# Gate and up products of a hybrid decoder trunk: eight quarter products per column tile, or seven by Strassen's scheme

## The chip, the cores and the metric

The kernel runs on one core of a Trainium2 chip (trn2). The metric is the device time of one execution in microseconds. Before the change it is 2174.89 us, the median of three runs (2173.87 to 2179.53).

## The reference

Two layers (DEPTH = 2) over 512 tokens of width 1024. Each layer runs two feed-forward blocks, a mixing sub-layer between them and a per-layer embedding at the end; the change touches the feed-forward blocks alone.

```python
def swiglu(x, wg, wu, wd):
    return (jax.nn.silu(x @ wg) * (x @ wu)) @ wd
...
#  h += 1/2 * post(SwiGLU_1(pre(h)))      pre and post: RMSNorm with a gain
#  h += post(mixing(pre(h)))
#  h += 1/2 * post(SwiGLU_2(pre(h)))
#  h += post(sigmoid(pre(h) @ W_g) * (p[i] @ W_p))
```

wg and wu are 1024 x 2816, wd is 2816 x 1024, all float32.

## The kernel before

Everything is kept transposed: channels in the 128 partitions, the 512 tokens in the columns. A product of float32 matrices is made of three products in the type float32r: each operand is split into a rounded high part and a rest, low part (`split`, `split_w`: ScalarE copies the high part, VectorE subtracts it), and `mm3` adds high x high, high x low and low x high in one PSUM bank.

A feed-forward block (`ffn`) has 22 column tiles (FT) of 128 hidden channels. For each tile, `gate_up` makes the gate and the up product: 8 row blocks (KD) of 128 channels times three partial products, 24 matmuls into a bank of the tag "mm" (four banks), for gate and up 48. The first three tiles are made in two token halves of 256 columns, so that they can start before the second half of the tokens is normalised; tiles 3 to 21 are 512 columns wide. The norm's gain is in the operand (`high`, `low`: xh, xl), its per-token scale r2 is put on the results afterwards, in `evacuate`: VectorE multiplies gate and up by r2 (L548, L550), ScalarE takes silu (L549), VectorE multiplies the two (L551) and the hidden tile is split for the next product (hh, hl: L200, L201). `evacuate` of a tile is called while the next tiles' matmuls run (`later`, `both`). Then `down` multiplies the 22 hidden tiles by wd into 8 output tiles, the last two again in token halves.

The weights come through `Weights`: chunks of 128 x 1024, eight 128 x 128 blocks, in one fixed list (`order`), a 512 KB DMA each from SyncE's queue (L55) into one of three buffers "raw", split by ScalarE (L185: wh) and VectorE (L186: wl) in two pieces of 512 columns, 12 buffers for each part. `part` calls `advance`, which runs four chunks ahead. A feed-forward block takes 44 chunks of gate and up (one of gate, one of up per tile, tiles in order) and 22 of down.

The order of the work is partly written by hand. Matmuls stay in program order (`in_order`), and after each of them chains that wait (norms, evacuations) go a step on when their time has come. `pin` and `front` keep the weight splits in order on ScalarE and VectorE. The rest is set by a scheduler at build time.

Of the kernel before, what the change touches and what calls it, by code (L numbers as in the profile page):

```python
# [20 lines left out]
FT = 22  # L21
HALF = 256
# [9 lines left out]
class Weights:  # L32
    """Streams [128, 1024] chunks of eight [128, 128] blocks and splits each into two float32r parts."""

    def __init__(self, kern, order, ahead):
        self.kern = kern
        self.order = order
        self.pos = {key: i for i, key in enumerate(order)}
        self.ahead = ahead
        self.issued = 0  # L40
        self.closed = {f"wo{l}" for l in range(L)}
        self.parts = {}
        self.base = None

    def advance(self, upto):
        k = self.kern
        while self.issued < min(upto, len(self.order)):
# [4 lines left out]
            raw = k.p_raw.tile([128, 1024], F32, tag="raw", name="raw")  # L52
            src = k.dram[name]
            if width == 512:
                self.last = k.nc.sync.dma_start(raw, src[c])  # L55
            else:
                self.last = k.nc.sync.dma_start(raw[:, :count * width], src[:, 3 * width * c:3 * width * c + count * width])
            part = []
            for i in range(count):
                if name.startswith("pp"):  # L60
                    hi, lo = (k.slot("big", n, dt=F32R) for n in ("pph", "ppl"))
                else:
                    hi = k.pool.tile([128, width], F32R, tag="wh", name="wh", bufs=12)
                    lo = k.pool.tile([128, width], F32R, tag="wl", name="wl", bufs=12)
                k.split_w(raw[:, width * i:width * i + width], hi, lo)
                part.append((hi, lo))
            self.parts[name, c] = part
            self.issued += 1

    def halves(self, name, c):  # L70
        """The two token halves, while the chunks from this one on have to stay for the second half."""
# [27 lines left out]
class Kern:  # L99
    def __init__(self, tc, ctx, dram, out):  # L100
        self.tc, self.nc, self.dram, self.out = tc, tc.nc, dram, out
        self.pool = ctx.enter_context(tc.tile_pool(name="sb", bufs=1))
        self.p_raw = ctx.enter_context(tc.tile_pool(name="raw", bufs=3))
# [3 lines left out]
        for l in range(L):  # L107
            order += [(f"gu{l}0", c) for c in range(44)] + [(f"dn{l}0", c) for c in range(22)]
            order += [(f"wi{l}", c) for c in range(8)] + [(f"wav{l}", c) for c in range(2)]
            order += [(f"wvg{l}", c) for c in range(3)] + [(f"wi{l}", c) for c in range(8, 14)] + [(f"wo{l}", c) for c in range(8)]  # L110
            order += [(f"gu{l}1", c) for c in range(44)] + [(f"dn{l}1", c) for c in range(22)]
# [9 lines left out]
        self.busy = False  # L121

# [10 lines left out]
    def after(self, ins, prev):  # L133
        """Keeps an instruction that is ready early from taking its tile long before it is needed."""
# [10 lines left out]
    def mm(self, out, lhs, rhs, start, stop):  # L145
        n = math.prod(out.shape[1:])
        self.in_order(self.nc.tensor.matmul(out, lhs, rhs, start=start, stop=stop),  # L147
# [5 lines left out]
    def in_order(self, ins, cycles):  # L153
        """Keeps the products in program order and lets waiting chains go on after each."""
# [23 lines left out]
    def drive(self, mark):  # L178
        """Emits the waiting chains up to a mark."""
# [3 lines left out]
    def split_w(self, src, hi, lo):  # L183
        """Never ahead of a step of a chain, or of an evacuation, that came before it."""
        for engine, ins in (("s", self.nc.scalar.activation(hi, src, AF.Copy)),  # L185
# [3 lines left out]
            self.pin(engine, ins, self.strict)  # L189

# [48 lines left out]
    def bias_table(self):  # L239
# [11 lines left out]
        ps = self.bank("o")  # L251
        self.mm(ps[:8], rb, oh, True, True)
        nc.vector.tensor_copy(row, ps[:8])
        ps = self.bank("o")
# [51 lines left out]
    def high(self, l, n, k, rng):  # L306
        """First float32r part of h times the norm's gain; the per-token scale follows the product."""
# [25 lines left out]
    def square_into(self, acc, src, last=False):  # L333
        """acc: the sum of the squares, and at the very end a last square that the product over the channels adds."""
# [16 lines left out]
    def start(self):  # L351
        """Loads x by pieces, in the order in which the first products need it and their weights."""
# [71 lines left out]
    def put_f(self, l, n, m, src, rng, square_first=False):  # L424
        """src None: the branch is there already, without the gain."""
# [12 lines left out]
    def finish(self, i, nxt, gain=None):  # L438
        """Adds the normalised branch to h over one token half, then prepares the next projection's operand."""
# [48 lines left out]
    def last_half(self, fs, bc, a, b):  # L488
        """The end of the last branch, with one pair of channel tiles on GpSimd."""
# [34 lines left out]
    def ffn(self, l, j, n_post, nxt):  # L524
# [57 lines left out]
        for mark in late:  # L582
            self.drive(mark)
# [671 lines left out]
```

## Time and profile before

| | |
|---|---|
| time, median of 3 runs | 2174.89 us |
| profiled execution: span, first to last instruction | 2176.8 us |
| profiled execution: own time | not given beside the span |
| PE busy (matmuls) | 2134.8 us, 98% |
| PE weight loads (PEld) | 1845.2 us, 85% |
| DVE (VectorE) busy | 1099.8 us, 51% |
| ACT (ScalarE) busy | 935.7 us, 43% |
| POOL (GpSimd) busy | 283.5 us, 13% |
| granted TensorE clock, mean | 0.995 of 2.4 GHz |
| DMA | 196.92 MB, 90 GB/s |

Busy time is the union of an engine's rows. Matmuls are pipelined, and a row lasts longer than the time until the next one starts; the price of a matmul is therefore read from the distance of starts. A weight load goes with each matmul and runs beside the one before. The chain of waits follows the end of the program back, at each step to what released it.

### The profile page before, as it was taken

To read this page: it belongs to the slowest core of one execution; us is meant where nothing else is said; L and a number is where in the kernel's file an instruction comes from. 1 tells how busy PE (TensorE), PEld (TensorE's weight loads), DVE (VectorE), ACT (ScalarE), POOL (GpSimd) and SP (SyncE) were. 2 spreads that over 40 slices of the span, in tenths; PEclk is the share of its full clock that TensorE was granted. 3 is DMA by queue.
4 is the path that set the end of the run, shared out by engine and by line. 5 is a ranking of instruction groups with operands and counts; after the bars stand their busy time and mean duration, and the time that the engine had idled before them with its cause. 6 is when DMAs were issued, how large, how long until landed. Compare 5 with 4: busy or idle time off the path is not lost.

```text
span 2176.8 us, 31253 instructions
## 1 busy us (share of the span) xinstructions
PE 2134.8 (98%) x12152; PEld 1845.2 (85%) x12152; DVE 1099.8 (51%) x2109; ACT 935.7 (43%) x1977; POOL 283.5 (13%) x392
## 2 busy tenths in 40 slices
PE   8999999999999999999999999999999999999998
PEld 7878888988989888889988888899989988888897
DVE  8444422767546444324774443246774564443264
ACT  5333322576744333324553333245675543333254
POOL 2000001312131000002320000022021410000032
PEclk9999999999999999999999999999999999999999
DMA  5342322441013232222232222324300232222221
GB/s 175 100 136 97 97 87 78 138 136 49 1 49 109 95 97 95 90 87 93 74 107 97 97 89 86 107 74 142 126 30 11 69 107 89 95 97 89 95 88 40
DMA packets 60684, 196.92 MB, mean 90 GB/s; under 512 B 6566, under 2 KB 10831, under 8 KB 60536
## 3 DMA queue, kind: packets, MB, share of 16 engines
q1 hardware_dynamic: 60536, 194.93, 27.5%
q8 instruction: 96, 1.57, 0.3%
q14 instruction: 52, 0.43, 0.1%
HBM read 192.78 MB, written 4.74 MB: 91 GB/s over the span
## 4 chain that ended last, share of the span: by engine, by line
PE 89%; DVE 5%; issue 2%; ACT 2%; POOL 1%; DMA 1%; DVEq 0%; SPq 0%; POOLq 0%; ACTq 0%
PE mm L147 80%; PE o L147 7%; PE t L151 2%; DVE wl L186 1%; PE t L147 1%; DVE xl L314 1%; DVE h L472 1%; POOL acc L344 0%; DMA raw<-in_pg 0%; DVE f L463 0%; ACT p L1115 0%; DVE f L466 0%; ACT wh L185 0%; POOL rs L299 0%; ACT xh L309 0%
## 5 line engine op out<-in xcount | busy, mean ns | idle before, releaser
L147 PE MATMUL mm<-xh,wh 128*128 128x512 f32 (+1 forms) x2112 | 753.3, 357 | 8.8 <-ACT wh L185 7.9
L147 PE MATMUL mm<-xl,wh 128*128 128x512 f32 (+1 forms) x2112 | 752.8, 356 | 6.9 <-DVE xl L314 6.8
L147 PE MATMUL mm<-xh,wl 128*128 128x512 f32 (+1 forms) x2112 | 751.3, 356 | 2.6 <-DVE wl L186 2.6
L186 DVE TENSOR_TENSOR wl<-raw,wh 128x512 fp32r<-128x512 f32 (+1 forms) x672 | 464.2, 706 | 543.3 <-ACT wh L185 541.6
L185 ACT ACTIVATE wh<-raw 128x512 fp32r<-128x512 f32 (+1 forms) x672 | 408.6, 631 | 629.6 <-PE mm L147 603.6
L147 PEld LDWEIGHTS mm<-xl,wh 128*128 128x128 f32 x2112 | 401.3, 190 | 71.5 <-DVE xl L314 10.7
L147 PEld LDWEIGHTS mm<-xh,wh 128*128 128x128 f32 x2112 | 401.3, 190 | 70.4 <-ACT wh L185 8.3
L147 PEld LDWEIGHTS mm<-xh,wl 128*128 128x128 f32 x2112 | 400.6, 190 | 64.7 <-DVE wl L186 3.7
L344 POOL TENSOR_TENSOR acc<-acc,sq 128x256 f32<-128x256 f32 x209 | 176.5, 855 | 1477.8 <-ACT sq L340 1473.5
L147 PE MATMUL mm<-hh,wh 128*128 128x512 f32 (+1 forms) x880 | 307.6, 350 | 0.0
L147 PE MATMUL mm<-hl,wh 128*128 128x512 f32 (+1 forms) x880 | 307.0, 349 | 0.0
L147 PE MATMUL mm<-hh,wl 128*128 128x512 f32 (+1 forms) x880 | 307.0, 349 | 0.0
L147 PEld LDWEIGHTS mm<-hl,wh 128*128 128x128 f32 x880 | 166.2, 189 | 24.2
L147 PEld LDWEIGHTS mm<-hh,wh 128*128 128x128 f32 x880 | 165.4, 188 | 24.1
L147 PEld LDWEIGHTS mm<-hh,wl 128*128 128x128 f32 x880 | 165.3, 188 | 23.9
L433 ACT ACTIVATE f<-mm,cols 128x256 f32<-128x256 f32 x96 | 46.2, 481 | 273.3 <-PE mm L147 273.2
L548 DVE TENSOR_TENSOR silu<-mm,r 128x512 f32<-128x512 f32 (+1 forms) x100 | 62.6, 626 | 129.9 <-PE mm L147 124.8
L550 DVE TENSOR_TENSOR up<-mm,r 128x512 f32<-128x512 f32 (+1 forms) x100 | 62.6, 626 | 125.6 <-PE mm L147 125.1
L200 ACT ACTIVATE hh<-silu 128x512 fp32r<-128x512 f32 (+1 forms) x100 | 57.8, 580 | 113.6 <-DVE silu L551 113.6
L314 DVE SCALAR_TENSOR_TENSOR xl<-h,cols,xh 128x256 fp32r<-128x256 f32 x128 | 85.4, 707 | 5.8 <-PE mm L147 3.6
L201 DVE TENSOR_TENSOR hl<-silu,hh 128x512 fp32r<-128x512 f32 (+1 forms) x100 | 62.4, 626 | 49.6 <-ACT hh L200 49.5
L1115 ACT ACTIVATE p<-p,mx 128x512 f32<-128x512 f32 (+3 forms) x128 | 70.3, 554 | 18.0 <-DVE mx L1111 18.0
(231 smaller groups left out, 2201.5 us busy)
## 6 DMA issues: line engine op xcount, KB each, us to landing
raw<-in_gu SPq DMA_DIRECT2D x176, 512.0 KB, 3.3
raw<-in_dn SPq DMA_DIRECT2D x88, 512.0 KB, 3.3
raw<-in_wi SPq DMA_DIRECT2D x28, 512.0 KB, 3.3
raw<-in_wo SPq DMA_DIRECT2D x16, 512.0 KB, 4.3
raw<-in_pg SPq DMA_DIRECT2D x16, 512.0 KB, 4.4
cw<-in_cw SPq DMA_DIRECT2D x16, 256.0 KB, 7.2
bias<-brow SPq DMA_DIRECT2D x16, 256.0 KB, 5.0
raw<-in_pp SPq DMA_DIRECT2D x6, 512.0 KB, 3.9
```

Of the source, the lines that this page charges most:

```text
L147: self.in_order(self.nc.tensor.matmul(out, lhs, rhs, start=start, stop=stop), n if lhs.dtype == F32R and n >= 256 else 4 * n)
L151: self.in_order(self.nc.tensor.transpose(out, src, self.ident), 256)
L185: for engine, ins in (("s", self.nc.scalar.activation(hi, src, AF.Copy)), ("v", self.nc.vector.tensor_sub(lo, src, hi.bitcast(F32)))):
L186: ("v", self.nc.vector.tensor_sub(lo, src, hi.bitcast(F32)))):
L200: nc.scalar.activation(hi, src, AF.Copy)
L201: nc.vector.tensor_sub(lo, src, hi.bitcast(F32))
L314: return self.nc.vector.scalar_tensor_tensor(lo, self.h[:, k, a:b], self.g[:, l, n, k:k + 1], hi.bitcast(F32), op0=OP.mult, op1=OP.subtract)
L344: nc.gpsimd.tensor_add(acc[0], acc[0], q)
L433: self.front["s"] = nc.scalar.activation(f, s, AF.Copy, scale=self.g[:, l, n, m:m + 1])
L548: nc.vector.tensor_mul(s, gu[0], r2[:, a:b])
L550: nc.vector.tensor_mul(u, gu[1], r2[:, a:b])
L1115: self.nc.scalar.activation(a["p"][i], a["p"][i], AF.Exp, bias=a["mx"][:, i:i + 1], accum_out=a["sm"][:, i:i + 1])
```

## The change

Tiles 6 to 21 (NC = 6) of each feed-forward block leave `gate_up` and go through `strassen`. For a column tile, gate above up is a matrix of two by two quarters: A11 and A12 are gate's row blocks 0 to 3 and 4 to 7, the lower pair are up's. The operand has quarters too: row blocks 0 to 3 or 4 to 7, token half left or right. Instead of eight quarter products, each 4 row blocks x 3 partial products of 256 columns, there are seven: A11 x B11, A12 x B21, S1 x t1, S2 x t2, S3 x T3, S4 x B22 and A22 x T4, where S, t and T are sums and differences of quarters (Winograd's form).

- `right_forms` makes the right-hand forms once per block, in the first six tiles, when the second token half's scale is there: h times gain times r2, complete, so that the per-token scale needs no place afterwards; then four differences per row-block pair and 14 splits in all, on VectorE and ScalarE (bh, bl).
- `Weights.form` replaces a tile's two chunk splits: loads of gate (g) and up (u), in steps "s1" and "s2" four additions of 512 columns on VectorE (L93: into y, u, y and z), then splits of g, y, u (1024 columns each) and z (512).
- `strassen` runs a tile's products interleaved with those of the tile before: A11(f), S4(f-1), A22(f-1), S2(f), A12(f), S3(f), S1(f). A tile has three half-filled banks: a ("mm"), b (one of the two "o" banks, in turn) and c ("mm"). ScalarE copies a into b after A11 (L764), so that S2, S1 and S4 add to it; b is read between them: after S2 (L781, up's left half), after S1 (L790, up's right half) and after S4 (L768, silu of gate's right half). Silu of gate's left half comes from a after A12 (L784). c gets S3, is added to up's right half (L791), then takes A22 x T4 and is added to up's left half (L772). L774 multiplies gate and up (up has its sign turned) into the hidden tile. Two one-matmul products per block write both b banks first.
- `evacuate` no longer splits the hidden tile. `split_hid` does it later: four tiles during `strassen`, 18 at the start of the down products, whose first two output tiles (`first_pair`) are now made row block by row block together.
- Buffers: eight of 1024 columns for raw chunks, y and all low parts ("raw"), six of 1024 for the high parts ("wh").

Where the instructions now stand: VectorE, a tile in the middle of the gate/up stage of a block, before (wl: low part of a weight piece; L548 to L551 and L201 as above):

```order
L186 TENSOR_TENSOR wl<-raw,wh 128x512
L548 TENSOR_TENSOR silu<-mm,r_99 128x512
L186 TENSOR_TENSOR wl<-raw,wh 128x512 x2
L550 TENSOR_TENSOR up<-mm,r_99 128x512
L186 TENSOR_TENSOR wl<-raw,wh 128x512
L551 TENSOR_TENSOR silu<-silu,up 128x512
L201 TENSOR_TENSOR hl<-silu,hh 128x512
```

and with the change:

```order
L93 TENSOR_TENSOR raw<-raw 128x512 x2
L791 TENSOR_TENSOR uv<-uv,mm 128x256
L93 TENSOR_TENSOR raw<-raw 128x512
L93 TENSOR_TENSOR sz<-raw 128x512
L250 TENSOR_TENSOR raw<-raw,wh 128x1024 x2
L772 TENSOR_TENSOR uv<-uv,mm 128x256
L774 SCALAR_TENSOR_TENSOR s<-uv,sg 128x512
L250 TENSOR_TENSOR raw<-raw,wh 128x1024
L250 TENSOR_TENSOR zl<-sz,zh 128x512
```

Eight instructions became eleven, and two of them (L791, L772) wait for products in the middle of the additions and splits for coming tiles.

ScalarE at the same place, before:

```order
L185 ACTIVATE wh<-raw 128x512 x2
L200 ACTIVATE hh<-silu 128x512
L185 ACTIVATE wh<-raw 128x512 x2
L549 ACTIVATE silu<-silu 128x512
L185 ACTIVATE wh<-raw 128x512 x4
```

and with the change:

```order
L790 ACTIVATE uv<-o 128x256
L764 ACTIVATE o<-mm 128x256
L249 ACTIVATE wh<-raw 128x1024
L249 ACTIVATE zh<-sz 128x512
L768 ACTIVATE sg<-o 128x256
L249 ACTIVATE wh<-raw 128x1024
L781 ACTIVATE uv<-o 128x256
L249 ACTIVATE wh<-raw 128x1024
L784 ACTIVATE sg<-mm 128x256
```

The copies that PE waits for (L764 before S2, L781 before S1, L790 before S4) stand between copies of high parts that wait for loads and additions.

SyncE's queue at the end of the first block's gate/up loads, before, with what each DMA waits for:

```order
L55 DMA raw_1603<-in_gu00 128x1024 [waits DMAHW6_49,DMAHW3_49,DVE_49]
L55 DMA raw_1648<-in_gu00 128x1024 [waits DMAHW4_49,DVE_49]
L55 DMA raw_1683<-in_gu00 128x1024 [waits DMAHW5_49,DVE_49]
L55 DMA raw_1728<-in_gu00 128x1024 [waits DMAHW6_49,DVE_49]
L55 DMA raw_1763<-in_gu00 128x1024 [waits DMAHW7_49,DVE_49]
```

and with the change:

```order
L82 DMA raw_2447<-in_gu00 128x1024 [waits DMAHW1_49,DVE_49]
L82 DMA raw_2568<-in_gu00 128x1024 [waits PE_49]
L82 DMA raw_2570<-in_gu00 128x1024 [waits DMAHW3_49,DVE_49]
L82 DMA raw_2691<-in_gu00 128x1024 [waits DMAHW0_49,PE_49]
L82 DMA raw_2693<-in_gu00 128x1024 [waits DMAHW5_49,DVE_49]
```

Loads of g (raw_2568, raw_2691) now wait for PE, loads of u (raw_2570, raw_2693) for VectorE. In the built program u's chunk takes the buffer of y of the tile before, once that y is split, and g's chunk one that a low part or the g of an earlier tile leaves.

The diff, cut to its core:

```diff
+NC = 6
...
+    def form(self, name, f, piece):
...
+        if piece == "load":
+            src = k.dram["gu" + name[2:]]
+            self.parts[name, f] = dict(g=self.fetch(src[2 * f]), u=self.fetch(src[2 * f + 1]))
+            return
...
+        if piece == "s1":
+            p["y"] = self.raw()
+            add(p["y"][:, lo], u[:, lo], u[:, hi])
+            add(u[:, lo], u[:, lo], g[:, lo])
+        elif piece == "s2":
+            p["z"] = k.slot("scr", "sz")
+            add(p["y"][:, hi], u[:, lo], u[:, hi])
+            add(p["z"], p["y"][:, hi], g[:, hi])
+        else:
...
+            last = k.split_w(t, h, low)
...
+    def ffn_order(l, j):
+        order = [(f"gu{l}{j}", c) for c in range(2 * NC)] + [(f"gs{l}{j}", (NC, "load"))]
+        for f in range(NC, FT):
+            order += [(f"gs{l}{j}", (f, piece)) for piece in ("s1", "s2", "g", "y")]
+            if f + 1 < FT:
+                order.append((f"gs{l}{j}", (f + 1, "load")))
+            order += [(f"gs{l}{j}", (f, piece)) for piece in ("u", "z")]
...
-            nc.vector.tensor_mul(s, s, u)
-            self.split(s, hid[f][0][:, a:b], hid[f][1][:, a:b])
+            nc.vector.tensor_mul(whole[f][:, a:b], s, u)
...
-        for f in range(3, FT):
+        for f in range(3, NC):
+            if f == NC - 2:
+                self.w.ahead = 9
             both(f, FULL)
...
-        for m in range(6):
+        self.strassen(l, j, forms, whole, split_hid)
+        first_pair()
+        for m in range(2, 6):
             down(m, FULL)
...
+    def right_forms(self, me, r2, forms):
...
+        for k in range(4):
+            a, b, c = (self.slot("big", "b") for _ in range(3))
...
+            times(a, k)
+            times(b, k + 4)
+            nc.vector.tensor_sub(c[:, left], b[:, right], a[:, right])
+            nc.vector.tensor_sub(a[:, right], a[:, left], a[:, right])
...
+            parts(a, ("B11", k), ("t1", k))
+            yield 2.0
+            parts(c, ("T3", k), ("t2", k))
+            parts(b, ("B21", k), ("B22", k))
...
+    def strassen(self, l, j, forms, whole, split_hid):
...
+        for b in shared:
+            p = w.parts[name, NC]
+            self.mm(b, p["A11"][0][:, :128], forms["B11"][0][0], True, True)
...
+                product(cur["a"], cur["p"], "A11", "B11", True)
+                nc.scalar.activation(cur["b"], cur["a"], AF.Copy)
+                pace(0)
+            if prev:
+                product(prev["b"], prev["p"], "S4", "B22")
+                nc.scalar.activation(prev["sg"][:, right], prev["b"], AF.Silu)
+                if cur:
+                    pace(1)
+                product(prev["c"], prev["p"], "A22", "T4")
+                nc.vector.tensor_add(prev["uv"][:, left], prev["uv"][:, left], prev["c"])
+                s = self.slot("big", "s")
+                nc.vector.scalar_tensor_tensor(s, prev["uv"], -1.0, prev["sg"], op0=OP.mult, op1=OP.mult)
...
+                product(cur["b"], cur["p"], "S2", "t2")
+                nc.scalar.activation(cur["uv"][:, left], cur["b"], AF.Copy)
+                pace(3)
+                product(cur["a"], cur["p"], "A12", "B21")
+                nc.scalar.activation(cur["sg"][:, left], cur["a"], AF.Silu)
+                pace(4)
+                cur["c"] = self.bank("mm")[:, :HALF]
+                product(cur["c"], cur["p"], "S3", "T3", True)
+                pace(5)
+                product(cur["b"], cur["p"], "S1", "t1")
+                nc.scalar.activation(cur["uv"][:, right], cur["b"], AF.Copy)
+                nc.vector.tensor_add(cur["uv"][:, right], cur["uv"][:, right], cur["c"])
...
-            a[f"dn{l}{j}"] = _blocks(ffn_w_down[l, j])
+            a[f"dn{l}{j}"] = _blocks(ffn_w_down[l, j], 2)
```

`pace(i)` sends the next piece of the weights' list (a load, an addition step or a split) after a product.

## Rows read from the trace of the kernel before

**Rows 1.** The page: busy time, share of the span and instructions of each engine.

```profile
PE 2134.8 (98%) x12152; PEld 1845.2 (85%) x12152; DVE 1099.8 (51%) x2109; ACT 935.7 (43%) x1977; POOL 283.5 (13%) x392
```

**Rows 2.** The page: the chain that ended last, shares by engine and by line.

```profile
PE 89%; DVE 5%; issue 2%; ACT 2%; POOL 1%; DMA 1%; DVEq 0%; SPq 0%; POOLq 0%; ACTq 0%
PE mm L147 80%; PE o L147 7%; PE t L151 2%; DVE wl L186 1%; PE t L147 1%; DVE xl L314 1%; DVE h L472 1%; POOL acc L344 0%; DMA raw<-in_pg 0%; DVE f L463 0%; ACT p L1115 0%; DVE f L466 0%; ACT wh L185 0%; POOL rs L299 0%; ACT xh L309 0%
```

**Rows 3.** Busy time by stretch: PE, PEld, DVE, ACT, POOL (instructions), granted clock, DMA share, GB/s.

```profile
629.00:647.00 18.00, 18.00 (x161) 18.00 (x160) 10.14 (x16) 10.31 (x28) 9.21 (x10) 1.00 0.13 42
676.00:720.00 44.00, 43.82 (x239) 37.57 (x240) 23.81 (x41) 18.03 (x32) 0.13 (x1) 1.00 0.39 131
800.00:930.00 130.00, 130.00 (x559) 104.75 (x558) 54.99 (x84) 41.02 (x68) 0.00 (x0) 1.00 0.29 94
```

**Rows 4.** Groups by shape: count | busy us, mean ns of one | idle before, releaser.

```profile
L147 PE MATMUL mm<-xh,wh 128*128 128x512 f32 x1344 | 532.7, 396 | 0.0
L147 PEld LDWEIGHTS mm<-xh,wh 128*128 128x128 f32 x2112 | 401.3, 190 | 70.4 <-ACT wh L185 8.3 <-DVE silu L548 1.1 <-issue 0.7
L186 DVE TENSOR_TENSOR wl<-raw,wh 128x512 fp32r<-128x512 f32 x656 | 457.8, 713 | 540.0 <-ACT wh L185 538.3
L185 ACT ACTIVATE wh<-raw 128x512 fp32r<-128x512 f32 x656 | 402.5, 636 | 625.4 <-PE mm L147 599.5 <-DMA raw<-in_pg 7.7 <-DMA raw<-in_gu 7.4
L548 DVE TENSOR_TENSOR silu<-mm,r 128x512 f32<-128x512 f32 x76 | 52.6, 692 | 123.5 <-PE mm L147 123.5
L551 DVE TENSOR_TENSOR silu<-silu,up 128x512 f32<-128x512 f32 x76 | 52.2, 686 | 0.0
L549 ACT ACTIVATE silu<-silu 128x512 f32<-128x512 f32 x76 | 48.1, 633 | 19.3 <-DVE silu L548 19.3
L551 DVE TENSOR_TENSOR silu<-silu,up 128x256 f32<-128x256 f32 x24 | 10.5, 442 | 0.3
L548 DVE TENSOR_TENSOR silu<-mm,r 128x256 f32<-128x256 f32 x24 | 10.1, 420 | 6.4 <-ACT r L322 4.8 <-PE mm L147 1.3
L549 ACT ACTIVATE silu<-silu 128x256 f32<-128x256 f32 x24 | 9.9, 413 | 7.9 <-DVE silu L548 7.6 <-ACT wh L185 0.2
```

**Rows 5.** Timeline of DVE, second block: start us, us, instruction [idle before].

```profile
693.42 0.69 DVE L548 TENSOR_TENSOR silu<-mm,r 128x512 f32<-128x512 f32 x1 [1.68 <-PE mm L147]
...
704.62 0.69 DVE L548 TENSOR_TENSOR silu<-mm,r 128x512 f32<-128x512 f32 x1 [1.63 <-PE mm L147]
...
715.82 0.69 DVE L548 TENSOR_TENSOR silu<-mm,r 128x512 f32<-128x512 f32 x1 [1.63 <-PE mm L147]
```

**Rows 6.** Timeline of PE before the second block, first and eleventh of eleven starts.

```profile
639.78 0.28 PE L147 MATMUL mm<-yh,wl 128*128 128x256 f32 x1
...
640.91 0.28 PE L147 MATMUL mm<-yh,wh 128*128 128x256 f32 x1
```

**Rows 7.** The chain of waits near the end of the program: start us, us.

```profile
2142.04 2.83 PE mm L147 x24
```

**Rows 8.** Timeline of ACT: the second half's scale r in the second block.

```profile
676.93 0.38 ACT L322 ACTIVATE r<-t 128x256 f32<-128x256 f32 x1 [0.59 <-PE t L147]
```

**Rows 9.** Timeline of DVE without pauses, four weight splits merged.

```profile
651.93 3.01 DVE L186 TENSOR_TENSOR wl<-raw,wh 128x512 fp32r<-128x512 f32 x4
```

**Rows 10.** The page: DMA issues, count, KB each, median us to landing.

```profile
raw<-in_gu SPq DMA_DIRECT2D x176, 512.0 KB, 3.3
...
raw<-in_pg SPq DMA_DIRECT2D x16, 512.0 KB, 4.4
cw<-in_cw SPq DMA_DIRECT2D x16, 256.0 KB, 7.2
```

**Rows 11.** Waits of PE: us in total, times, longest.

```profile
PE o L147 <- ACT pj L636: 1.5, 2, 0.8
```

More of the change, by code (lines that the diff above doesn't have):

```diff
@@ L51, in advance @@
             width, count = (280, 2 if c == 2 else 3) if name.startswith("wvg") else (512, 2)
-            raw = k.p_raw.tile([128, 1024], F32, tag="raw", name="raw")
+            if name.startswith("gs"):
+                self.form(name, *c)
+                self.issued += 1
+                continue
             src = k.dram[name]
[L54 to L57, printed above, removed]
+            raw = self.fetch(src[c]) if width == 512 else self.fetch(
+                src[:, 3 * width * c:3 * width * c + count * width], count * width)
@@ L65, in advance, with raw, fetch @@
-                k.split_w(raw[:, width * i:width * i + width], hi, lo)
+                    hi, lo = wh[:, cols], wl[:, cols]
+                last = k.split_w(raw[:, cols], hi, lo)
                 part.append((hi, lo))
+            if wh is not None:
+                self.first.append(last)
             self.parts[name, c] = part
             self.issued += 1
+    def raw(self, dt=F32):
+        return self.kern.p_raw.tile([128, 1024], dt, tag="raw", name="raw")
+    def fetch(self, src, cols=1024):
+        k, t = self.kern, self.raw()
+        self.last = k.nc.sync.dma_start(t[:, :cols], src)
+        if len(self.first) > 1:
+            k.after(self.last, self.first.pop(0))
+        return t
@@ new lines, in high @@
+    def high(self):
+        return self.kern.pool.tile([128, 1024], F32R, tag="wh", name="wh", bufs=6)
+    def form(self, name, f, piece):
+        k = self.kern
+        add = lambda o, a, b: k.pin("v", k.nc.vector.tensor_add(o, a, b))
+        if piece == "load":
+            src = k.dram["gu" + name[2:]]
+            self.parts[name, f] = dict(g=self.fetch(src[2 * f]), u=self.fetch(src[2 * f + 1]))
+            return
+        p = self.parts[name, f]
+        lo, hi = slice(0, 512), slice(512, 1024)
+        g, u = p["g"], p["u"]
+        if piece == "s1":
[7 more added lines that the diff above has]
+        else:
+            t = p[piece]
+            if piece == "z":
+                h = k.pool.tile([128, 512], F32R, tag="zh", name="zh", bufs=2)
+                low = k.slot("scr", "zl", dt=F32R)
+            else:
+                h, low = self.high(), self.raw(F32R)
+            last = k.split_w(t, h, low)
+            if piece in ("g", "y"):
+                self.first.append(last)
+            for i, n in enumerate({"g": ("A11", "A12"), "y": ("S1", "S2"), "u": ("S3", "A22"), "z": ("S4",)}[piece]):
+                cols = slice(512 * i, 512 * i + 512)
+                p[n] = (h[:, cols], low[:, cols])
@@ L573, in ffn, with split_hid, first_pair @@
                 both(f, rng)
[L574 removed]
+        for f in range(3, NC):
+            if f == NC - 2:
+                self.w.ahead = 9
             both(f, FULL)
[L576 to L581 removed]
+        self.w.ahead = 4
         for mark in late:
             self.drive(mark)
+        self.drive(f"b{me}")
         self.begin_f(("big", "scr"))
+        def split_hid(k):
+            hid[k] = (self.slot("big", "hh", dt=F32R), self.slot("big", "hl", dt=F32R))
+            self.split(whole.pop(k), *hid[k])
+        def first_pair():
+            banks = [self.bank("mm") for _ in range(2)]
+            for k in range(FT):
+                if k in whole:
+                    split_hid(k)
+            for k in range(FT):
+                for m in range(2):
+                    ah, al = self.w.block(f"dn{l}{j}", 2 * k + m)
+                    bh, bl = hid[k]
+                    self.mm(banks[m], ah, bh, k == 0, False)
+                    self.mm(banks[m], ah, bl, False, False)
+                    self.mm(banks[m], al, bh, False, k == FT - 1)
+            for m in range(2):
+                self.put_f(l, n_post, m, banks[m], FULL)
         def down(m, rng):
```

105 lines of the change are left out of this document (85 added, 20 removed).

## The prediction

> **What bounds the kernel now.** I read the page first. TensorE (PE) is busy for 98% of the span, VectorE (DVE) for 51% and ScalarE (ACT) for 43% [rows 1]. Busy PE is no proof that PE is the limit, so I read the chain of waits next: 89% of it is PE, and 80% are matmuls into the "mm" banks [rows 2]. The stretches then show one gate/up stage from inside: from 800 to 930 us PE and its clock are full (granted clock 1.00, the 2.4 GHz level), DVE is busy 55 of 130 us, ACT 41, GpSimd not at all [rows 3]. So in this stage a matmul saved is time saved, as long as DVE and ACT, which have 58% and 68% free, can take what the change gives them.
>
> What one column tile costs is read from the timeline. DVE takes up each tile's gate bank at 693.42, 704.62 and 715.82 us [rows 5]: **11.20 us a tile**, with 48 matmuls of 512 columns (2 matrices, 8 row blocks, 3 partial products), 0.2333 us each. The rows' mean of 396 ns [rows 4] isn't the price: matmul rows overlap.
>
> **The price of a 256-column matmul.** Two rates stand in the trace, both with a new weight load for each product. In one stretch ten products start within 640.91 - 639.78 = 1.13 us, 0.113 each [rows 6]; in another 24 take 2.83, 0.118 each [rows 7]. Nothing in these rows tells me which rate a new stage gets, so both are kept: 84 products (7 times 4 row blocks times 3) take 84 x 0.113 = 9.49 us or 84 x 0.118 = 9.90 us. I take 9.90, since the waits that I can't see lie on that side too.
> The Trainium skill has a price for this as well: "TensorE: Matmul & The Clock Gate", section Back-to-back issue gap, gives columns / 2.4 + 2.5 ns at full clock, so 216 ns for 512 columns and 109 for 256. By it (an estimate) a tile would go from 10.36 to 9.17 us, and 64 tiles would give 76 us instead of the 83 below. The trace disagrees at 512 columns (0.233 a matmul), and the measurement decides.
>
> **The sum, part by part.**
> - Matmuls: 16 tiles in each of 4 blocks. 64 x (11.20 - 9.90) = **83 us less**; at the faster rate 64 x 1.71 = 109.
> - Two extra seed products per block: 8 x 0.118 = 0.9 us more.
> - Edges: the first tile has no older tile's products to run while ACT copies bank a into bank b (its S2 waits), and the last tile's S4 waits for ACT to empty b. The nearest row is PE waiting for ACT to empty a bank: twice, 1.5 us together, 0.8 at most [rows 11]. 2 x 4 x 0.8 = 6.4 us more. Inside the stage the same copies lie beside one product (12 x 0.118 = 1.4 us, for the copy before S4) or two (2.8 us), against an ACT copy of 0.41 [rows 4], so they cost nothing; without that cover each would cost the 0.8.
> - DVE per tile: four adds of 512 at 0.686, three splits of 1024, one of 512 at 0.713, two adds of 256 at 0.42 and one combination of 512 at 0.69. From 256 to 512 columns a row grows from 442 to 686, 0.244 per 256 [rows 4], so a 1024 split is put at 0.713 + 2 x 0.244 = 1.20. Sum 2.74 + 3.60 + 0.71 + 0.84 + 0.69 = **8.6 us of 9.5 to 9.9** (before: 4 x 0.713 + 4 x 0.69 = 5.6 of 11.2). Rows overlap by 0.09 when DVE runs without a pause: four splits in 3.01 [rows 9], so its true need is about 7.6. Covered, with little to spare; if not covered, the excess over PE's 9.5 to 9.9 is paid 64 times.
> - ACT per tile: three copies of 1024 (0.636 + 2 x 0.220 = 1.08), one of 512 at 0.64, five of 256 at 0.41 to 0.42 [rows 4]: 5.9 us (before: 4 x 0.636 + 2 x 0.63 = 3.8). Covered. But its queue is in order: a copy that waits for g's load stands ahead of the two that empty the banks for S4 and S2.
> - Entry: the right-hand forms must be ready when tile 5 ends. The second half's scale is there at 676.93 [rows 8], tile 5's gate bank is full at 715.8 and its up bank 5.6 later, at 721.4: 44 us. DVE does 23.8 us in that stretch now [rows 3]; without the nine hidden splits (three of 0.69, six of 0.42) 19.2. Forms add, per pair of row blocks, 2 x 0.69 + 4 x 0.42 + 3.5 x 0.69 = 5.5, four times 22; tile 6's own operands 2.7 + 3.6 + 0.7 = 7.0. Together 48 by durations, about 42 with the overlap of [rows 9]. It just fits; the rows that follow tile 5's gate bank are few. Taken at 0; ends 0 and 5 us per block.
> - Hidden splits, now after the stage: 18 at 0.69 = 12 us of DVE in the first pair of down products, which lasts 22 x 6 x 0.233 = 31 us and asks for a new one each 1.4 us; the first four are made earlier. 0. If they are late, PE waits for the fifth row block.
> - Fewer buffers for raw chunks and low halves together (8 of 1024 columns, before 3 raw and 12 low halves of 512) in the other stages: 0. A load is 3.3 us [rows 10] and a chunk is eaten in 5.6 or, in the half-width stretches, 2.8. What it costs without that cover is in the range.
> - Loads: the same bytes, but u of the tile after next is loaded only after DVE has split y (the SP rows above). This loop is u's landing, two adds, the bank's add, two adds, g's split, y's split: 4 x 0.69 + 0.42 + 2 x 1.20 = 5.6 us by durations. With a landing of 3.3 it is 8.9; with 4.4, as where chunks follow each other closely [rows 10], 10.0. Tiles 6 and 7 are made ahead, and a loop that is late holds up the bank's add first, whose bank isn't written again before A11 and S4 are over, 2.8 us after S1. Taken at 0; the end is 10.4 us a tile.
>
> Sum: -83 + 0.9 + 6.4 = **-75.7 us**. The profiled span is 2176.8; no time of that execution is given beside it, but the three runs (2173.9 to 2179.5) lie on both sides of it, so nothing is added around it. 2176.8 - 75.7 = 2101.1, which is 1.9 less against the median of 2174.9: **2099 us**.
>
> **Rivals.**
> 1. The faster rate holds: 2174.9 - 109 + 7 = 2073. For it: the rows at 640 us hold that rate [rows 6]. It is the lower end.
> 2. The operands bound the stage. DVE, ACT and the load loop have cover of one microsecond or less, so a tile may come at 10.2 to 10.9 instead of 9.9. At 10.4: -64 x 0.8 + 7 = -44, 2131. For it: DVE at 8.6 with waits on PE in the middle of its queue. Against: the overlap of DVE's rows, and the tiles made ahead.
> 3. **Slower:** the load loop. g and u of one tile are asked for at nearly the same time, and if they hinder each other, u's landing goes to what slow transfers here show, 7.2 us [rows 10]; the loop is then 5.6 + 7.2 = 12.8 and 64 x 1.6 + 7 = +109, 2284. It decides from a landing of 5.6 us, where the loop is as long as the old tile. Against: a gu chunk of the same size lands in 3.3, pg's close followers in 4.4.
> 4. The change doesn't give what its count says, because a product of 256 columns is priced by its weight load. A load's row stretches over the whole of a 256-column stretch: 18.00 of 18 us, against 104.75 of 130 at 512 columns [rows 3]. If loads came one after another at the 190 ns of their rows [rows 4], a tile would take 84 x 0.190 = 16 us and the kernel 2480. Against it: a load goes with every product there, at 0.113 to 0.118 [rows 6, 7]. Break-even is 11.2 / 84 = 0.133. Behind this rival stands a rule of the Trainium skill ("Perfetto Trace Analysis", section Identifying the Most-Contended Engine): TensorE's headroom is judged by the weight loads' busy share, not by the matmuls'. By it 48 loads at 81% would leave room for some 60 in the old tile's time, not for 84; the trace has the 81% and the 100%, but also 24 loaded products in 2.83 us, so the share isn't a price here.
>
> **Chances and range.** My forecast (PE sets the pace at 0.118) 0.45, rival 1 0.18, rival 2 0.25, rival 3 0.08, rival 4 or an exact balance 0.04. About 0.3%, 6.5 us, is what a measurement of this kernel tells from no change. Faster by more: 0.88; within: 0.03; slower: 0.09. The range goes from rival 1 to rival 2 with some entry wait added (2131 + 2 per block): **2072 to 2138**.
>
> **What would show it.** Right: in the new profile PE starts 84 products per tile within 9.5 to 9.9 us, DVE is 75 to 90% busy there, and PE waits show two waits for ACT of about 0.8 us per block. Wrong: waits of PE's products for the second addition into uv, for ACT's copy of g, or for DVE's forms, 0.3 us or more in each tile (rival 2); SP's loads of u landing after 5 us (rival 3); products at over 0.125 us without any wait (rival 4); long waits of the first product of a block for the forms (entry).

## The result and the profile after

The changed kernel takes 2146.41 us (median of 4 runs, 2145.8 to 2147.23) against 2175.54 of the kernel before in the same runs: ratio 0.9865, 95% interval 0.9851 to 0.9879. It is 29 us faster; 2099 was predicted, with 2138 as the upper end. The profiled span falls from 2176.8 to 2144.6 us.

The page after, engines and the chain that ended last, the answer to [rows 1, 2]:

```profile
PE 2082.0 (97%) x14464; PEld 1918.7 (89%) x14464; DVE 1389.1 (65%) x2505; ACT 1076.7 (50%) x2277; POOL 278.2 (13%) x392
...
PE 65%; DVE 19%; DMA 10%; ACT 4%; issue 2%; POOL 0%; SPq 0%; DVEq 0%; ACTq 0%; POOLq 0%
PE mm L211 51%; PE o L211 10%; DMA raw<-in_gu 9%; DVE raw L250 6%; DVE raw L93 4%; DVE xl L379 2%; PE t L215 2%; PE t L211 2%; DVE sz L93 1%; DVE h L537 1%; ACT wh L249 1%; DVE f L528 1%; DVE uv L791 1%; DMA raw<-in_dn 0%; ACT xh L374 0%
...
raw<-in_gu SPq DMA_DIRECT2D x176, 512.0 KB, 3.6
```

PE is still busy nearly all the time, but 29% of the chain now runs through DVE and DMA, mostly the loads of gate and up: in the new stage the loop of u's load and DVE's work on it takes as long as PE. Two of its loads in the chain, 9.90 us apart, which is also the price of 84 products at 0.118:

```profile
796.80 4.23 DMA raw<-in_gu
...
806.70 4.66 DMA raw<-in_gu
```

Inside the stage the forecast holds. Timeline of PE after, the first product of tile 6 in the second block and the first down product behind the stage:

```profile
722.67 0.41 PE L211 MATMUL o<-bh,wh 128*128 128x256 f32 x2
...
884.92 0.40 PE L211 MATMUL mm<-hh,wh 128*128 128x512 f32 x1
```

That is 162.3 us for 16 tiles, 10.1 each with the edges, instead of 16 x 11.20 = 179.2 [rows 5]. Busy time by stretch, in the columns of [rows 3], and PE's waits in this stage (us in total, times, longest):

```profile
800.00:880.00 80.00, 79.05 (x669) 78.64 (x668) 62.39 (x86) 41.24 (x75) 0.00 (x0) 1.00 0.36 108
...
PE o L211 <- ACT uv L790: 1.3, 2, 0.9
PE o L211 <- ACT o L764: 0.5, 1, 0.5
```

Where the time went, from such first and last starts (us; "between" is everything from the last down product to tile 6 of the next block, so norms, mixing or embedding, and tiles 0 to 5; before, tile 6 is put 179.2 ahead of the first down product):

| | start | new stage, blocks 1, 2, 3, 4 | down, 1, 2, 3, 4 | between 1-2, 2-3, 3-4, end |
|---|---|---|---|---|
| before | 88.2 | 179.2 each | 123.7, 124.1, 123.7, 124.7 | 330.1, 138.8, 330.6, 76.2 |
| after | 85.3 | 174.3, 162.3, 160.9, 161.8 | 125.9, 126.0, 125.7, 126.0 | 337.1, 142.9, 339.4, 76.9 |
| difference | -2.9 | -57.5 together | +7.6 together | +20.6 together |

Three things stand out: block 1's stage gains 5 us and not 17; the down products, which the change hardly touches, are slower; the stretches between, which hold none of the new products, lose 20 us.

**The down products** have no waits. The chain of waits in a stretch of them (start us, us, what) shows another distance of starts; first before, then after:

```profile
904.78 20.30 PE mm L147 x87
```

```profile
889.78 22.38 PE mm L211 x95
```

20.30 / 87 = 0.2333 us, 22.38 / 95 = 0.2356. The half-width products changed too: before 53 in 6.02 (0.1136) or, in other stretches, 45 in 5.30 (0.1178); after 69 in 8.29 (0.1201), all from the chain:

```profile
1001.94 6.02 PE mm L147 x53
...
1012.76 5.30 PE mm L147 x45
```

```profile
985.90 8.29 PE mm L211 x69
```

**Between**, the largest single loss is in the mixing stage. PE's waits after, from 425 to 440 us, and what ACT and DVE do before (timelines):

```profile
PE o L211 <- issue: 2.7, 1, 2.7
```

```profile
409.81 1.15 ACT L249 ACTIVATE wh<-raw 128x512 fp32r<-128x512 f32 x2
413.55 1.16 ACT L249 ACTIVATE wh<-raw 128x512 fp32r<-128x512 f32 x2 [2.60 <-DMA raw<-in_wi]
416.35 1.16 ACT L249 ACTIVATE wh<-raw 128x512 fp32r<-128x512 f32 x2 [1.65 <-DMA raw<-in_wav]
419.32 1.16 ACT L249 ACTIVATE wh<-raw 128x512 fp32r<-128x512 f32 x2 [1.81 <-DMA raw<-in_wav]
```

```profile
419.99 1.30 DVE L250 TENSOR_TENSOR raw<-raw,wh 128x512 fp32r<-128x512 f32 x2 [1.68 <-ACT wh L249]
421.20 0.69 DVE L975 TENSOR_TENSOR xb<-mm,r 128x512 f32<-128x512 f32 x1
```

DVE takes up the bank xb only when it has split a chunk (wav) that is needed much later and has just landed. Everything in front of the convolution shifts, and PE waits 2.7 us: the profile names no releaser for this wait, but the operand xc that it ends with is written by DVE's row

```profile
431.70 0.75 DVE L1089 SCALAR_TENSOR_TENSOR xc<-xb,cols,xc 128x511 f32<-128x511 f32 x1
```

**Block 1's stage**: the chain there runs through the transfers that spread the bias rows (brow), which the change moved with the bias table from gate tiles 5 and 7 to tiles 7 and 9, into the new stage, and PE waits for what hangs on the late load:

```profile
130.69 5.49 DMA brow<-rows
...
136.25 10.01 DMA raw<-in_gu
```

```profile
PE o L211 <- ACT uv L781: 5.4, 1, 5.4
```

That load takes 10.0 us, where the others of this stage take 3.4 to 4.8. And the wait has a tail: in it the granted clock falls to 0.50, the 1.2 GHz level, and the first 16 products behind it start 0.213 apart instead of 0.118, 1.6 us more. Busy time by stretch, in the columns of [rows 3]:

```profile
146.50:153.30 6.80, 3.47 (x16) 3.47 (x17) 5.24 (x7) 3.58 (x7) 0.00 (x0) 0.50 0.29 83
```

**The clock.** The profiles have such stretches at 0.50 elsewhere too: leaving out the first 40 and the last 20 us of the program, two before the change (at 651 and 1727 us) and five after it (at 147, 433, 1037, 1488 and 1710). If each product that starts in one is charged what its distance exceeds 0.117 or 0.233 us, they cost 3.7 us before and 9.5 after (an estimate from these traces): some 6 of the 47 us that are missing to 2099.

### The profile page after: what moved, and what is told of

Read it like the earlier page. It is cut to its first block, busy times and chain, and to the rows that moved or that the text cites. A ratio compares the mean times of both kernels' runs of the same rounds, so it can differ in the third digit from the quotient of the medians.

```text
span 2144.6 us, 36353 instructions
## 1 busy us (share of the span) xinstructions
PE 2082.0 (97%) x14464; PEld 1918.7 (89%) x14464; DVE 1389.1 (65%) x2505; ACT 1076.7 (50%) x2277; POOL 278.2 (13%) x392
## 4 chain that ended last, share of the span: by engine, by line
PE 65%; DVE 19%; DMA 10%; ACT 4%; issue 2%; POOL 0%; SPq 0%; DVEq 0%; ACTq 0%; POOLq 0%
PE mm L211 51%; PE o L211 10%; DMA raw<-in_gu 9%; DVE raw L250 6%; DVE raw L93 4%; DVE xl L379 2%; PE t L215 2%; PE t L211 2%; DVE sz L93 1%; DVE h L537 1%; ACT wh L249 1%; DVE f L528 1%; DVE uv L791 1%; DMA raw<-in_dn 0%; ACT xh L374 0%
## 5 line engine op out<-in xcount | busy, mean ns | idle before, releaser
L250 DVE TENSOR_TENSOR raw<-raw,wh 128x512 fp32r<-128x512 f32 (+2 forms) x608 | 520.0, 881 | 370.2 <-ACT wh L249 359.0
L249 ACT ACTIVATE wh<-raw 128x512 fp32r<-128x512 f32 (+2 forms) x608 | 438.8, 763 | 395.9 <-DMA raw<-in_gu 128.6
L211 PE MATMUL mm<-xh,wh 128*128 128x256 f32 (+1 forms) x1088 | 351.2, 323 | 9.5 <-ACT wh L249 7.8
L211 PE MATMUL mm<-xl,wh 128*128 128x256 f32 (+1 forms) x1088 | 348.9, 321 | 9.0 <-DVE xl L379 8.6
L211 PE MATMUL mm<-xh,raw 128*128 128x256 f32 (+1 forms) x1088 | 348.6, 320 | 2.5 <-DVE raw L250 2.5
L211 PE MATMUL mm<-hh,raw 128*128 128x512 f32 (+1 forms) x880 | 310.3, 353 | 0.0
L211 PE MATMUL mm<-bh,wh 128*128 128x256 f32 x1024 | 289.0, 282 | 3.1 <-DVE uv L791 3.0
L211 PE MATMUL mm<-bh,raw 128*128 128x256 f32 x1024 | 287.9, 281 | 0.0
L211 PE MATMUL mm<-bl,wh 128*128 128x256 f32 x1024 | 287.3, 281 | 0.0
L211 PEld LDWEIGHTS mm<-xh,wh 128*128 128x128 f32 x1088 | 208.5, 192 | 25.6 <-ACT wh L249 8.2
L211 PEld LDWEIGHTS mm<-xh,raw 128*128 128x128 f32 x1088 | 207.9, 191 | 19.1 <-DVE raw L250 3.6
L93 DVE TENSOR_TENSOR raw<-raw 128x512 f32<-128x512 f32 x192 | 132.3, 689 | 86.0 <-DMA raw<-in_gu 84.0
```

Of the source, the lines that this page charges most:

```text
L93: add = lambda o, a, b: k.pin("v", k.nc.vector.tensor_add(o, a, b))
L250: ("v", self.nc.vector.tensor_sub(lo, src, hi.bitcast(F32)))):
```

## The experiments

**The buffers alone (e1, e5).** e1 is the kernel before with the new `advance`, `fetch`, `high` and eight raw tiles; e5 keeps low halves and raw chunks apart:

```diff
 e1: raw pool bufs=3 -> 8; wh [128, 512] x12 -> [128, 1024] x6
-    lo = k.pool.tile([128, width], F32R, tag="wl", name="wl", bufs=12)
+    wl = k.p_raw.tile([128, 1024], F32R, tag="raw", name="raw")
 e5: raw pool stays 3
+    wl = k.pool.tile([128, 1024], F32R, tag="wl", name="wl", bufs=6)
```

> The kernel before with nothing of the seven products, only the new weight buffers (high halves in six tiles of 1024 columns, low halves in the same eight tiles as the raw chunks, loads tied to the second last split). Theory B (the buffers cost what the new kernel loses outside its new stage): matmuls of 512 columns at 235.5 ns instead of 233.4, those of 256 at 118 to 120 instead of 113 to 118, each down stage 125.9 us instead of 123.7 to 124.7, each mixing stage 7 to 9 us longer, the whole some 30 us slower than the kernel before, about 2205. Rival S (the losses follow from the new stage itself, its order or what it leaves behind): the cadence stays at 233.4 and the time at 2175, within 4 us.

> The kernel before with its high and its low halves in six tiles of 1024 columns each instead of twelve of 512 (one tile for both halves of a chunk), and its three raw tiles as before: nothing is shared between raw chunks and low halves, there are nine such tiles instead of eight, and high and low halves start 32 bytes off a multiple of 64, as before. Theory C (it is the count: eight tiles for raw chunks and low halves together make loads late in the mixing stages): cadence and time as before, 2176 within 5 us. Theory W (it is the width: a split of a chunk waits until the whole old tile is free, and stands ahead of evacuations on the in-order queues): some 10 to 15 us over the kernel before, 2187 to 2190, like the shifted shared tiles.

Measured: e1 2210.53 us, ratio 1.0156 (1.0135 to 1.0177). Theory B: the new buffers without any of the seven products cost 33 us, more than the whole change gains. Down stages 125.6 to 125.9, the stretches with mixing +7.1 and +10.7, 512 columns at 0.2355:

```profile
902.88 27.32 PE mm L162 x116
```

e5 takes 2181.94, ratio 1.0029 (1.0020 to 1.0038), 7 us over before and between its two theories: with the old cadence (87 in 20.30) the wide tiles, together with the tie of a load to the second last split, which e5 has too, cost these 7 us. The rest of e1's 33 came with the sharing, which also moves the low halves to another place in memory.

**The place of the low halves (e2, e3, e6, e11, e13).** The build puts the operands 34144 bytes into a partition's memory plus multiples of 2048; the high halves start 64 bytes behind an operand's start modulo 256, before and after. The low halves started 64 behind it too, and in the new buffers 32 (z's low half, of the new stage alone, starts as an operand does in every changed kernel). Each of these kernels moves them, and but for a memset or two the instructions and their order stay the same on every engine:

```diff
 e2, in e1:    raw tile [128, 1040], used from column 8
 e3, in after: a pool of [128, 8] ahead of the raw pool
 e6, in after: e3, and [128, 8] ahead of all operands
 e11, in before: a tile [128, 8] between the tiles wh and wl
 e13, in after: e3 with [128, 16]
```

> The same with each raw tile 1040 columns wide and used from column 8, so that the low halves start 32 bytes off a multiple of 64 bytes, as the high halves and the operands do (before they did too; in the new buffers the low halves start on a multiple of 64). Theory A (the cadence depends on where in its 64 bytes a low half starts): 512 columns back at 233.4 ns, 256 back at 113 to 118, some 15 to 20 us less than the run with the plain new buffers. Rival (it is the sharing of the tiles, the width or the phase in which the products meet): cadence and time as in that run, within 4 us.

> The new kernel with its pool of raw chunks and low halves moved by 32 bytes. Theory A: the down stages back from 125.9 to about 124, the matmuls of 512 columns at 233.4 ns; the whole at 2146 - 18 = about 2128. Rival: 2146 within 4 us, 512 columns at 235.5.

> The new kernel with everything in place so that operands, high halves and low halves all start on a multiple of 64 bytes (raw and low tiles did; the others are moved by 32 bytes). Theory A1 (what counts is that a weight tile and the operand start alike within 64 bytes): the cadence falls to 233.4 and 113 to 118 as in the run with the pool moved by 32 bytes, about 2136. Theory A2 (a multiple of 64 is bad in itself, for whatever is read): all three products of a block get slower, 512 columns above 235.5, the time above 2150. Theory A3 (a multiple of 64 is better, and only the mixture was bad): 512 columns below 233, the time below 2130.

> The kernel before, instruction for instruction in the same order on every engine, with 32 unused bytes between the tiles of the high halves and those of the low halves, so that low halves start on a multiple of 64 bytes while high halves and operands lie 32 bytes beside one. Theory A: 512 columns go from 233.2 to 235.3 ns (5800 of them, 12 us) and 256 from 116.2 to about 118.7 (4080, 10 us): about 2198, with each down stage near 125.9. Rival (the start within 64 bytes matters only with tiles of 1024 columns or a shared pool): 2176 within 4 us, cadence as before.

> The new kernel with its pool of raw chunks and low halves moved by 64 bytes: the low halves start on a multiple of 64 again, but 96 bytes behind an operand's start in a period of 256, where they were 32 behind (new kernel) and 64 behind (pool moved by 32). Theory P (the rate follows this distance, as the kernel before with 32 bytes put in at the same distance of 96 shows): 512 columns at 231.1 ns, 256 outside the new stage at 118.4, so against the run moved by 32 (2135.9) some 2700 x 2.2 ns = 6 us less and 4000 x 2.4 ns = 10 us more: about 2140. Theory A (a multiple of 64 is what slows them): 235.5 ns and 2146.

Measured (mean distance of starts in ns, over all neighbouring products of equal width, those with a wait left out; the 256 column includes the new stage where there is one):

| kernel | low behind operand, bytes mod 256 | 512 columns | 256 columns | time us | ratio to before |
|---|---|---|---|---|---|
| before | 64 | 233.2 | 116.2 | | |
| e1 | 32 | 235.2 | 118.8 | 2210.53 | 1.0156 (1.0135 to 1.0177) |
| e2 | 0, 64, 128, 192 in turn | 232.3 | 116.4 | 2189.05 | 1.0058 (1.0036 to 1.0081) |
| after | 32 | 234.9 | 118.5 | 2146.41 | 0.9865 (0.9851 to 0.9879) |
| e3 | 64 | 233.1 | 116.1 | 2135.93 | 0.9808 (0.9787 to 0.9829) |
| e6 | 64 | 233.1 | 115.7 | 2134.66 | 0.9808 (0.9793 to 0.9823) |
| e11 | 96 | 231.1 | 118.4 | 2170.80 | 0.9972 (0.9961 to 0.9982) |
| e13 | 96 | 231.1 | 118.6 | 2138.24 | 0.9824 (0.9808 to 0.9840) |

The same in the chains of down products, e3, e11, e13 in this order, and e11 at half width:

```profile
884.99 27.07 PE mm L212 x116
```

```profile
904.93 20.11 PE mm L149 x87
...
995.96 8.34 PE mm L149 x70
```

```profile
889.80 22.42 PE mm L212 x97
```

The place is worth 21 us in the kernel with the buffers alone (e2), and 10 us in the changed one (e3, 32 bytes): there theory A had expected 18. But its rule was wrong. In e6 the low halves are back on a multiple of 64, with everything else, and the time and cadence of e3 stay, as A1 had it. In e11 the low halves start on a multiple of 64 as in e1, high halves and operands do not, and 512 columns got faster: 2171, where theory A said 2198 and its rival 2176. What fits all eight kernels is the distance (theory P), and e13, forecast by it, came out at 2138 for 2140, with 231.1 for 231.1 and 118.6 for 118.4. In e2, whose eight tiles lie at four distances in turn, the mean of 24 products (one chunk) in the down stages goes from 231.0 to 233.3 chunk by chunk, where e1 stays at 235.5 or 235.6. It is a rule read from these rows. In all eight kernels the high halves lie 64 bytes behind the operands, so whether the distance to the operand or the one to the high halves counts is not shown, nor is what in the chip makes it so.

**The bias rows (e4, e7, e12).** In e4 the eight transfers are written behind the third down tile; e7 is e4 with e3's pool. e12 also ties them behind a load of the down chunks:

```diff
 e4, e7 (and a yield in the table's program ahead of the transfers):
+            if (l, j, m) == (0, 0, 2):
+                next(self.table, None)
 e12, in e9 below:
-            nc.sync.dma_start(d, ...)
+            self.load(d, ...)
```

> The new kernel with the eight transfers that spread the bias rows (brow) issued in block 1's down stage instead of its new stage. Theory D (these transfers hold up the loads of g and u, which stand in a loop with the splits): the new stage of block 1 falls from 174.2 to about 163 us, as in the other blocks (160.7 to 162.1), the whole from 2146 to about 2135. Rival (block 1 is slower for another reason, the softplus or its entry): 174 and 2146, within 3 us.

> The new kernel with both repairs that helped alone: the pool moved by 32 bytes and the transfers of the bias rows in the down stage. If the two are independent: 2146 - 10.5 - 5.4 = about 2130; if the stage of block 1 is bound by its operands either way: 2134 to 2136.

> The run with both repairs and the look-ahead of three in the mixing stages (2118.6), with the transfers of the bias rows tied behind a load of the down stage. In e4 and the runs after it they were written later in the program, but the scheduler had put them back into the new stage, at 130 to 137 us, with two loads of gate and up between them instead of none. Theory D: out of the stage, block 1's new stage falls from 166 to 169 us to 161 or 162, as in the other blocks, and the whole to about 2113. Rival (the rest of block 1's delay, whose waits begin at 104 us, before these transfers, is of its first tiles): 165 and 2117, within 3 us.

e4: 2141.06, ratio 0.9835 (0.9818 to 0.9852), block 1's stage 168.2. It didn't do what it was meant to: the scheduler put the transfers back at 130.7 to 137.1 us, only with two loads of gate and up between them, so what it tests is this. Of the 6.1 us that the stage gains, 1.7 are the clock, which stays at 1.00 there. e7: 2128.07, 0.9776 (0.9760 to 0.9792); the two repairs add up as expected. In e12 the transfers are issued at 283 to 288 us: 2113.78, 0.9713 (0.9697 to 0.9730), the forecast 2113, but in part by luck: block 1's stage takes 164.3, where 161 or 162 was expected and e9 has 166.2, and in the two profiles another 2.8 us of the difference lie in the second stretch with mixing, which e12 doesn't touch and where e9's clock fell twice. The stage's waits:

```profile
PE mm L212 <- DVE uv L796: 3.1, 3, 1.3
PE o L212 <- ACT uv L795: 0.5, 1, 0.5
PE o L212 <- ACT o L769: 0.5, 1, 0.5
```

The 5.4 us behind the late load are gone; three waits for the addition into uv stay, and with them about 3 us.

**The look-ahead (e8, e9).** Both start from e7:

```diff
 e8:
-        self.w = Weights(self, order, 4)
+        self.w = Weights(self, order, 3)
 and 3 again behind the gate tiles; e9 only:
+            self.w.ahead = 3
             self.mixing(l, (l, 4))
+            self.w.ahead = 4
```

> The last one with a look-ahead of three chunks instead of four in the plain stages, so that a chunk's splits are put into the queues of ScalarE and VectorE later. Theory Q (splits that wait for a tile or a load stand ahead of the evacuations in the mixing stages, and cost the 5 us before the convolution's products): mixing is 3 to 5 us shorter in each layer, the whole 6 to 10 us less than that run. Rival (loads are late for lack of tiles, and a shorter look-ahead makes it worse): equal or up to 15 us more.

> Both repairs (pool moved by 32 bytes, bias rows spread in the down stage), and the look-ahead of three chunks in the two mixing stages alone, four elsewhere. By the stages of the run with three everywhere: mixing gains 7.4 and 12.0 us, and the 4.9 and 4.4 us that were lost behind the second and the fourth block come back: 2128 - 19 = about 2109. Rival (the shorter look-ahead pays in the mixing stage only because what comes before or after it is late too): about 2117, as with three everywhere.

e8: 2116.67, ratio 0.9732 (0.9715 to 0.9749), 11 us less than e7. The stretches with mixing fall from 337.2 and 341.2 to 329.8 and 329.1, to what they took before the change. That is more than theory Q's 3 to 5 us each. In the trace of the first, from 405 to 440 us PE waits for nothing, and DVE takes up xb behind one landing of wav instead of two:

```profile
407.26 1.16 ACT L250 ACTIVATE wh<-raw 128x512 fp32r<-128x512 f32 x2 [1.86 <-DMA raw<-in_wav]
```

```profile
407.92 1.29 DVE L251 TENSOR_TENSOR raw<-raw,wh 128x512 fp32r<-128x512 f32 x2 [1.72 <-ACT wh L250]
409.13 0.69 DVE L980 TENSOR_TENSOR xb<-mm,r 128x512 f32<-128x512 f32 x1
```

The second wav chunk is now split behind the evacuations; the first still stands in front of xb, so the mechanism is weaker and not gone: xb follows ACT's row for the scale r by 8.8 us, against 11.7 in the changed kernel and 7.2 before. In the profiles of e7 and e8 the 7.4 and 12.1 us are in the main PE's waits (3.9 and 5.6 less) and products started at the lower clock (2.6 and 6.5 us less by the count above; e8's clock stays at 1.00 in both stretches).

The embeddings lost 4.9 and 4.4 us against e7. Part of that is the shorter look-ahead: right behind the second and the fourth down stage PE waits 3.1 us for a weight's split, 0.7 in e7, and 0.7 again in e9, where it is four there. Still e9 takes 2118.61, 0.9733 (0.9717 to 0.9749), not 2109: the stretches with embeddings stay at 143.7 and 80.4, those with mixing take 331.6 and 333.6. In the last stretch, behind the fourth block, every engine has the same instructions in the same order in e7 and e9, and PE has the same waits. What differs is the clock, 25.6 us behind the last down product, e7 and then e9 (busy time by stretch, as above):

```profile
2078.00:2084.80 6.80, 6.80 (x62) 6.80 (x61) 2.85 (x7) 2.77 (x7) 0.71 (x1) 1.00 0.25 77
```

```profile
2063.40:2070.20 6.80, 6.80 (x34) 6.80 (x33) 0.16 (x1) 0.28 (x1) 0.71 (x1) 0.50 0.25 77
```

Level until then, e9 comes out of it 3.2 us late and stays so for the next 30 us and more. In both, a wait of 1.84 us ends just before; why the clock fell in one execution and not in the other, no run here shows. So these stage times, each of one execution, can differ by some 3 us without any difference in the program.

**The softplus (e10)**, moved behind the fourth down tile in e9:

> The same with the softplus (26 small instructions of VectorE at 0.16 us) in block 1's down stage too. Theory V (VectorE's queue has so little room that small instructions hold up the tile's chain): the new stage of block 1 falls from 169 to about 165 us, the whole by 4 more, about 2105. Rival (block 1 is late for its loads alone): 169 and no change within 2 us.

2117.19, ratio 0.9736 (0.9712 to 0.9759), block 1's stage 168.8 for 166.2. The scheduler put the softplus not into the down stage but at 234 to 248 us, at the new stage's end, where it had stood at 117 to 144 among the late tiles; these got no faster without it. Theory V falls.

## Why the prediction was right and wrong

- **The bound, and the new stage: right in blocks 2 to 4.** 84 products at 0.118 are 9.90 us; the stages of blocks 2 to 4 took 160.9 to 162.3, with 158.4 + 0.2 + 1.6 = 160.2 forecast. DVE is busy 62.39 of 80 us there, 78%, ACT 41.24; the edges are the waits shown, 1.8 us. Rival 4 (the price of a weight load) is out, and so is rival 3: loads land in 3.6, those of u on the chain in 4.2 and 4.7, where it decides from 5.6.
- **The load loop at 8.9 to 10.0: right, and closer than I made of it.** In e3 block 4's stage ran at 0.114 in many stretches, where 84 products would need 9.6, and took 159.2, 9.95 a tile. There the load loop sets the pace for a time, 9.65 us from load to load, as rival 2 had it, but only below PE's 9.9. Its chain:

```profile
1865.42 3.99 DMA raw<-in_gu
...
1875.07 4.04 DMA raw<-in_gu
```

- **Entry and hidden splits at 0: right.** Tile 6's first product follows tile 5's last at 0.24 us (722.43 to 722.67), and with the cadence restored (e3) a down stage takes 124.1 to 124.7.
- **The step that failed: "Fewer buffers for raw chunks and low halves together in the other stages: 0."** e1 measures it alone: 33 us, against 75.7 of expected gain. I priced only the cover of a load (3.3 us, measured 3.6), but three other things hang on a buffer. Its place: two thirds of e1's loss and 10 us of the changed kernel's. Its width: 7 us in e5, which doesn't separate it from the tie of the loads; that a chunk's two splits now wait for one tile together is argued from the program, no trace was read for it. And its order: with four chunks of look-ahead, splits that wait for a landing stand ahead of evacuations on ACT and DVE (e2, with about the old cadence: 4.8 and 6.0 us more in the two stretches with mixing; e8: 7.4 and 12.1 back, some half of it PE's waits and most of the rest products at the lower clock).
- **Two terms that were missing.** The bias table and its eight transfers moved into a stage whose loads stand in a loop with the splits. The text prices no such thing; of block 1's shortfall of 12 us e4 takes back 6.1 and e12 brings the stage to 164.3. And the sum holds the clock at full speed throughout: after the change it loses some 6 us more at 0.50 than before.
- With the place, the order and the bias rows repaired the time is 2113.78 us (e12), faster than both kernels. Its span is 62 us under before's, 14 short of the 76: the new stages give 68 (block 1's still lacks 3), the stretches with the embeddings cost 9 (7 of them products started at the lower clock, which the profile of before has none of there), those with mixing 2, and the start gives back 5.

## What to carry to other kernels

A change of buffers is a change in every stage that uses them: build it alone, without the gain it is for, and time it. Read the distance of matmul starts in a stage that the change doesn't touch; if it moved, look where the tiles start in memory. And look for what else a moved piece of program takes along into the new stage: a transfer that was hidden beside a deep look-ahead isn't hidden in a loop. Before a difference of a few microseconds in a stage is put down to an edit, compare the granted clock of that stage in the two profiles.

## What the runs showed of the hardware

The place of a weight tile against the operand changed the distance of starts by up to 4 ns in 233 and 3 in 118, with the same instructions in the same order (e1 to e13, the table above); the best distance for 512 columns (96) is not the best for 256 (64).

At one and the same place there are also two rates. Timeline of PE in the kernel before, down products of the first block:

```profile
375.78 0.28 PE L147 MATMUL mm<-hh,wh 128*128 128x256 f32 x1
...
376.57 0.28 PE L147 MATMUL mm<-hl,wh 128*128 128x256 f32 x1
376.69 0.28 PE L147 MATMUL mm<-hh,wl 128*128 128x256 f32 x1
376.80 0.50 PE L147 MATMUL t<-const,acc 128*128 128x1 f32 x4
377.16 0.36 PE L147 MATMUL mm<-hh,wh 128*128 128x256 f32 x1
377.36 0.28 PE L147 MATMUL mm<-hl,wh 128*128 128x256 f32 x1
...
378.54 0.28 PE L147 MATMUL mm<-hh,wl 128*128 128x256 f32 x1
```

Ahead of the four one-column products of a norm the starts are 0.113 apart (nine in 1.02 us), behind them 0.118 (ten in 1.18), and they stay so for the rest of that stage. In the last block's down products it is the other way round, 0.118 ahead (twelve in 1.41) and 0.114 behind (eight in 0.91):

```profile
2084.59 0.28 PE L147 MATMUL mm<-hh,wh 128*128 128x256 f32 x1
...
2086.00 0.50 PE L147 MATMUL t<-const,acc 128*128 128x1 f32 x4
...
2086.57 0.28 PE L147 MATMUL mm<-hl,wh 128*128 128x256 f32 x1
...
2087.48 0.28 PE L147 MATMUL mm<-hh,wh 128*128 128x256 f32 x1
```

So the rate can change at such an interruption, either way; what decides it is not shown. These are the two rates that [rows 6] and [rows 7] had shown. The 256 column of the table above is a mean over both.

The Trainium skill ("TensorE: Matmul & The Clock Gate", section Back-to-back issue gap) gives some 216 ns for 512 columns and 109 for 256 by a formula for a product by itself, and some 131 ns at 512 columns for a stream of weight loads and products; the prediction names only the first. No stage here came below 231.1 and 113.3, with a weight load for each product, so the first comes nearer, and the trace agrees with neither.
